# RWKV-7 chunk chain: the decayed old state added on VectorE in the state's update, in place of an identity product on TensorE

## Chip, cores, metric

One core of a Trainium2 chip. The metric is the device time of one execution in microseconds (us). The engines are called as in the profile: PE is TensorE (PEld its weight loads), DVE is VectorE, ACT is ScalarE, POOL is GpSimd, SP is SyncE, which here only issues DMAs.

## What is computed

One decoder layer on 512 tokens of 2048 channels, in fp32. Its sub-layer normalises and modulates x, projects it with a 2048 x 12416 matrix, mixes the time axis in two branches (RWKV-7 and a short convolution), gates both, projects them back and adds the result to x. What the change touches is the recurrence of RWKV-7, for 16 heads of 64 channels:

```python
def step(S, inp):
    r_t, w_t, k_t, v_t, kk_t, b_t = inp
    sa = jnp.einsum('bhvk,bhk->bhv', S, -kk_t)
    S = (S * w_t[:, :, None, :] + sa[..., None] * b_t[:, :, None, :]
         + v_t[..., None] * k_t[:, :, None, :])
    y_t = jnp.einsum('bhvk,bhk->bhv', S, r_t)
    return S, y_t
...
pa = pa + (shift_time(pa, 1) - pa) * mu_shift[l]     # pa: the projected columns of r, k, v
y_a = (rwkv7_mix(pa, ...) * jax.nn.silu(z_a)) @ p_a[l]
```

## The kernel before

The time axis is cut into NC = 8 chunks of 64 tokens, and the heads are taken in NP = 8 pairs; a pair fills the 128 partitions, one head on each half (the two slices in `halves`). Inside a chunk the recurrence is solved in closed form, and only the state goes from chunk to chunk. The generator `chunks(j, ...)` does this for pair j, and its loop over c (lines 870 to 901) is the serial chain that the change is about. `SB` holds two state buffers in SBUF, and each step reads S0 and writes S1. A step consists of these parts:

- `o1` (a 128 x 128 corner of PSUM bank tag "pc") is GK·VB (L877) plus AR·S0 (L879). AR·S0 is the first instruction that needs the new state.
- `o2` (PSUM bank tag "py") is Kt·VB (L883) plus ident·S0 (L885), the old state passed through an identity matrix so that it lands in the accumulator.
- ACT copies the two diagonal 64 x 64 blocks of o1 to `UB` (L888), and PE adds Z·UB to o2 (L890).
- ACT writes S1 as o2 times `end`, the decay over the chunk, in two 64 x 64 blocks (L895).

Each of these fp32 products stands in the trace as two rows of PE. The chain's steps 1 to 6 have the identity product (48 in all), steps 1 to 7 have AR·S0 (56 in all).

All of this runs inside a large dense projection: `dense()` (L1018 to L1044) multiplies h with the projection matrix, 128 x 512 columns at a time (L1036), from weights that ACT and POOL split into a high and a low part (`high`, `low`). A planner written in the kernel merges the streams: it steps a clock `now` by the books' cost of each PE instruction (`spend`), lets each side generator run when its time has come, and writes the instructions down in that order, one queue for each engine. `run(engine, cost, ...)` (L422) books an operation on ACT, DVE or POOL and writes it down at most SOON = 1.2 us ahead; its line L428 is therefore the line of nearly all work on these engines, and the text goes by the names of the tiles. After an operation that PE needs, a generator waits for its booked end plus HOP + SURE = 0.2 + 0.6 us before it writes the PE instruction down. Work of the next pair (`prepare`, `invert`) uses DVE at the same time as the chain of this pair: `invert` is a long row of small dependent DVE operations with names `invt`, `Xg`, `M`.

Of the kernel before, what the change touches and what calls it, by code (L numbers as in the profile page):

```python
# [11 lines left out]
AF = mybir.ActivationFunctionType  # L12
ALU = mybir.AluOpType
# [12 lines left out]
NC = T // C  # L26
# [50 lines left out]
def trunk(ctx: ExitStack, tc: tile.TileContext, xT_d, x_d, prm_d, crow_d, ada1_d, ada2_d, rows_d, w_d, lora_d, pa_d, pb_d,  # L77
          wo_d, out_d):
    nc = tc.nc
    V, A, G, TE, S = nc.vector, nc.scalar, nc.gpsimd, nc.tensor, nc.sync  # L80
# [26 lines left out]
    ident = cst.tile([P, P], F32, name="ident")  # L107
# [78 lines left out]
    with tc.tile_pool(name="ap", bufs=1) as ap, tc.tile_pool(name="psa", bufs=1, space=PSUM) as psa:  # L186
# [189 lines left out]
        while units or opened:  # L376
# [3 lines left out]
            if u is None and units and len(opened) < NOPEN:  # L380
                b, t, k0, n = units[0]
# [8 lines left out]
            b, t, ps, k0, n, i = u  # L390
# [20 lines left out]
    with tc.tile_pool(name="rp", bufs=1) as rp, tc.manual_schedule(engines=ALL):  # L411
# [6 lines left out]
        def spend(t):  # L418
            nonlocal now
            now += t  # L420

        def run(eng, cost, f, *args, **kw):  # L422

            two = eng in ("POOL", "DVE2")
            e = eng[:3] if eng == "DVE2" else eng
            while busy[e] > now + SOON:
                yield busy[e] - SOON
            f(*args, **kw)  # L428
            t = max(now, busy[e])
            if two:  # L430
                while port and port[0][1] <= now:
                    port.pop(0)
                for b, c in port:
                    if b < t + cost and t < c:
                        t = c
                port.append((t, t + cost))
                port.sort()
            busy[e] = t + cost
            return busy[e] + HOP
# [11 lines left out]
        def take(tag, name, n=T):  # L451
            while books[tag][0][0] is None or books[tag][0][0] > now:
                yield now + 0.25 if books[tag][0][0] is None else books[tag][0][0]
            books[tag].pop(0)
            book = [None]
            books[tag].append(book)
            return bank(tag, name, n), book

        def four(ps):
            return ps.rearrange("p (a b) -> p a b", a=4)  # L460
# [358 lines left out]
        def chunks(j, AR, GB, GK, bon, end, vpad, solved, **_):  # L819
# [24 lines left out]
            for c0, m in ((0, 4), (4, 4), (8, 1)):  # L844
# [6 lines left out]
                for h, b in enumerate(halves):  # L851

                    k0, k1 = max(c0 + h - 1, 0), min(c0 + m + h - 1, NC)
                    if k0 < k1:
                        w0 = k0 + 1 - h - c0
                        t = yield from run("ACT", 0.38, A.activation, VB[b, k0:k1, b], pv[b, w0:w0 + k1 - k0, b], AF.Copy)
# [13 lines left out]
            for c in range(NC):  # L870
                if c % 4 == 0:
                    p1, b1 = yield from take("pc", f"p1{n}_{c}")
                    p2, b2 = yield from take("py", f"p2{n}_{c}")
                    p1, p2 = four(p1), four(p2)
                o1, o2 = p1[:, c % 4, :], p2[:, c % 4, :]
                S0, S1 = SB[:, c % 2, :], SB[:, (c + 1) % 2, :]
                TE.matmul(o1, GK[:, c, :], VB[:, c, :], start=True, stop=(c == 0))  # L877
                if c:
                    TE.matmul(o1, AR[:, c, :], S0, start=False, stop=True)  # L879
                spend(0.44)  # L880

                if c < NC - 1:
                    TE.matmul(o2, Kt[:, c, :], VB[:, c, :], start=True, stop=False)  # L883
                    if c:
                        TE.matmul(o2, ident, S0, start=False, stop=False)  # L885
                    spend(0.44)
                for b in halves:
                    t = yield from run("ACT", 0.22, A.activation, UB[b, b], o1[b, b], AF.Copy)  # L888
                yield t + SURE
                TE.matmul(o2, Z[:, c, :], UB, start=(c == NC - 1), stop=True)  # L890
                spend(0.22)
                yield now + SUM
                if c < NC - 1:
                    for b in halves:
                        t = yield from run("ACT", 0.3, A.activation, S1[b, b], o2[b, b], AF.Copy, scale=end[b, c:c + 1])  # L895
                if c % 4 == 3:
                    for h in range(NH):
                        b, o = halves[h], halves[1 - h]
                        b1[0] = yield from run("ACT", 0.38, A.activation, yt[o, c - 3:c + 1, :], p1[o, :, b], AF.Copy)
                        b2[0] = yield from run("ACT", 0.38, A.activation, y2[o, c - 3:c + 1, :], p2[o, :, b], AF.Copy)  # L900
                yield t + SURE
# [166 lines left out]
        for i in range(NFULL):  # L1068
            for t, f in USES:
                due.append([0.0, f(i, first[t + i], [None])])  # L1070
        sides = [[g, 0.0] for g in (
            high(), low(), loader(), uses(soon), uses(due),
            side("chunks", lambda j: "solved" in ops[j] and "bon" in ops[j], lambda j: chunks(j, **ops[j])),
            side("ops", paced, lambda j: prepare(j, rkv[j], ops[j])),
            side("inv", lambda j: at["made"] > j, lambda j: invert(j, out=ops[j], **ops[j])),
# [270 lines left out]
```

## Time and profile before

| | |
|---|---|
| three runs | 1649.26, 1649.77, 1641.44 us (median 1649.26) |
| the profiled execution | 1647.3 us, of which the span of its instructions 1645.0 us |
| PE busy | 1610.1 us (98%) |
| DVE, ACT, POOL busy | 887.9 (54%), 654.5 (40%), 808.7 us (49%) |
| dense stage with the chains of the eight pairs | about 199 to 1257 us of the span |

The busy time of PE is the union of its rows, whose ends are modelled, so the pitch from the start of one row to the start of the next says more about cost than the length of a row. Times in a timeline count from the start of the span. The arrow in brackets names what ended the idle time of the engine.

### The profile page before, as it was taken

What the parts mean: (1) busy time and instruction counts of PE and PEld (TensorE: products, weight loads), DVE (VectorE), ACT (ScalarE), POOL (GpSimd) and SP (SyncE); (2) the same over time, 40 slices, a digit from 0 to 9 for tenths busy, and PEclk for the clock granted to TensorE, in tenths of its full rate; (3) what the DMA queues carried; (4) which work ended last, traced back from release to release, by engine and by line L of the source; (5) the groups of instructions that cost most, each with busy time, mean ns of one, the idle gap of its engine ahead of it and who ended that gap; (6) DMA issues with size and microseconds to landing.
All of it is one profiled execution on the core that took longest, in us unless ns stands there. A gap on an engine that the chain in (4) does not pass through costs nothing. (4 is left out here: it accounts for less than half of the span.)

```text
span 1645.0 us, 23157 instructions
## 1 busy us (share of the span) xinstructions
PE 1610.1 (98%) x8248; PEld 1325.5 (81%) x8248; DVE 887.9 (54%) x1548; ACT 654.5 (40%) x1363; POOL 808.7 (49%) x649
## 2 busy tenths in 40 slices
PE   6999999999999999999999999999999999999997
PEld 2778878888888888888888888888887887888885
DVE  3898287863868736826927687340201344544405
ACT  4555352424545235335345452344423223323411
POOL 1599565553434533544534445333444445775421
PEclk6999999999999999999999999999999999999998
DMA  7986334333322333343333234433443776665704
GB/s 259 396 324 256 91 106 124 103 103 100 95 87 82 102 110 87 102 116 97 115 102 101 77 98 120 113 108 97 136 152 109 233 239 191 204 208 171 239 26 154
DMA packets 138885, 235.72 MB, mean 143 GB/s; under 512 B 34833, under 2 KB 43665, under 8 KB 134673
## 3 DMA queue, kind: packets, MB, share of 16 engines
q1 hardware_dynamic: 138624, 234.15, 45.2%
q8 instruction: 65, 1.06, 0.3%
q14 instruction: 50, 0.41, 0.1%
q10 hardware_dynamic: 146, 0.09, 0.0%
HBM read 214.79 MB, written 19.14 MB: 142 GB/s over the span
## 5 line engine op out<-in xcount | busy, mean ns | idle before, releaser
L428 POOL TENSOR_TENSOR wL_c<-raw_c,wH_c 128x512 fp32r<-128x512 f32 x324 | 438.1, 1353 | 544.9 <-ACT wH_c L428 504.4
L1036 PE MATMUL ps_c<-hH,wL_c 128*128 128x512 f32 x1296 | 512.5, 395 | 0.6 <-POOL wL_c L428 0.6
L1036 PE MATMUL ps_c<-hH,wH_c 128*128 128x512 f32 x1296 | 512.8, 396 | 0.0
L1036 PE MATMUL ps_c<-hL,wH_c 128*128 128x512 f32 x1296 | 512.8, 396 | 0.0
L428 ACT ACTIVATE wH_c<-raw_c 128x512 fp32r<-128x512 f32 x324 | 204.3, 631 | 410.3 <-PE ps_c L1036 285.4
L1036 PEld LDWEIGHTS ps_c<-hH,wL_c 128*128 128x128 f32 x1296 | 243.8, 188 | 48.1 <-POOL wL_c L428 1.1
L1036 PEld LDWEIGHTS ps_c<-hH,wH_c 128*128 128x128 f32 x1296 | 243.7, 188 | 47.7
L1036 PEld LDWEIGHTS ps_c<-hL,wH_c 128*128 128x128 f32 x1296 | 243.7, 188 | 46.7
L149 POOL TENSOR_TENSOR fL<-fraw,fH 128x512 fp32r<-128x512 f32 x56 | 80.0, 1437 | 61.8 <-ACT fH L148 61.7
L428 DVE TENSOR_TENSOR invt<-M,Xg 128x60 f32<-128x60 f32 (+24 forms) x248 | 87.2, 351 | 42.3 <-DMA M<-s 34.6
L149 POOL TENSOR_TENSOR oL<-wo,oH 128x512 fp32r<-128x512 f32 x48 | 66.2, 1386 | 59.9 <-ACT oH L148 58.5
L160 PE MATMUL fps<-hH,fH 128*128 128x512 f32 x224 | 88.5, 395 | 4.1 <-ACT hH L259 4.1
L161 PE MATMUL fps<-hL,fH 128*128 128x512 f32 x224 | 88.5, 395 | 1.9 <-DVE hL L262 1.9
L162 PE MATMUL fps<-hH,fL 128*128 128x512 f32 x224 | 88.2, 394 | 1.7 <-POOL fL L149 1.7
L428 DVE TENSOR_TENSOR Xg<-Xg,invt 128x60 f32<-128x60 f32 (+24 forms) x248 | 83.9, 338 | 8.0
L428 DVE TENSOR_TENSOR GG<-pg,gmask 128x512 f32<-128x512 f32 x32 | 22.1, 692 | 109.5 <-PE pg L730 109.5
L245 DVE SCALAR_TENSOR_TENSOR ada<-ada,csr 128x2048 f32<-128x2048 f32 x32 | 72.6, 2276 | 13.9 <-PE csr L273 13.9
L160 PE MATMUL po<-oH,mH 128*128 128x512 f32 x192 | 74.7, 389 | 0.0
L161 PE MATMUL po<-oL,mH 128*128 128x512 f32 x192 | 74.7, 389 | 0.0
L162 PE MATMUL po<-oH,mL 128*128 128x512 f32 x192 | 74.7, 389 | 0.0
L148 ACT ACTIVATE oH<-wo 128x512 fp32r<-128x512 f32 x64 | 38.4, 627 | 74.1 <-PE po L162 46.7
L149 POOL TENSOR_TENSOR wL_pb<-raw_pb,wH_pb 128x512 fp32r<-128x512 f32 x32 | 41.3, 1292 | 49.4 <-ACT wH_pb L148 49.4
(268 smaller groups left out, 2599.5 us busy)
## 6 DMA issues: line engine op xcount, KB each, us to landing
raw_c<-in_w_dram SPq DMA_DIRECT2D x324, 256.0 KB, 2.7
ada<-in_ada_dram SPq DMA_DIRECT2D x32, 1024.0 KB, 8.8
gr<-in_ada_dram SPq DMA_DIRECT2D x64, 256.0 KB, 4.4
wo<-in_wo_dram SPq DMA_DIRECT2D x64, 256.0 KB, 3.7
fraw<-in_w_dram SPq DMA_DIRECT2D x56, 256.0 KB, 4.1
raw_pb<-in_pb_dram SPq DMA_DIRECT2D x32, 256.0 KB, 2.7
raw_pa<-in_pa_dram SPq DMA_DIRECT2D x32, 256.0 KB, 2.8
th_s<-th SPq DMA_DIRECT2D x30, 256.0 KB, 2.0
```

Of the source, the lines that this page charges most:

```text
L148: A.activation(H, src, AF.Copy)
L149: eng.tensor_tensor(L, src, H.bitcast(F32), ALU.subtract)
L160: TE.matmul(ps, wH, xH, start=start, stop=False)
L161: TE.matmul(ps, wH, xL, start=False, stop=False)
L162: TE.matmul(ps, wL, xH, start=False, stop=stop)
L245: V.scalar_tensor_tensor(ada[j, i], ada[j, i], 0.5, csr, ALU.mult, ALU.mult, accum_out=accs[j][:, i:i + 1])
L428: f(*args, **kw)
L1036: TE.matmul(ps, w[:, i, :], x[k], start=(k == k0 and x is hH and w is H), stop=(k == KT - 1 and w is L))
```

## The change

The identity product L885 goes. The old state is decayed on its own: ACT scales S0 by `end` into S1, the full 128 x 128 buffer in one instruction (steps 1 to 6, written down right behind the copies to UB), and DVE then adds the rest in place, S1 = o2 · end + S1, in two 64 x 64 blocks. In step 0, where there is no old state, DVE writes S1 = o2 · end. ACT's two blocks of L895 are thereby gone in all seven steps. The books change with it: 0.22 us for each product, and in step 0 the second product that was booked and did not exist is no longer booked.

```diff
-                spend(0.44)
+                spend(0.44 if c else 0.22)
 
                 if c < NC - 1:
                     TE.matmul(o2, Kt[:, c, :], VB[:, c, :], start=True, stop=False)
-                    if c:
-                        TE.matmul(o2, ident, S0, start=False, stop=False)
-                    spend(0.44)
+                    spend(0.22)
                 for b in halves:
                     t = yield from run("ACT", 0.22, A.activation, UB[b, b], o1[b, b], AF.Copy)
+                if 0 < c < NC - 1:
+                    yield from run("ACT", 0.4, A.activation, S1, S0, AF.Copy, scale=end[:, c:c + 1])
                 yield t + SURE
                 TE.matmul(o2, Z[:, c, :], UB, start=(c == NC - 1), stop=True)
                 spend(0.22)
                 yield now + SUM
                 if c < NC - 1:
                     for b in halves:
-                        t = yield from run("ACT", 0.3, A.activation, S1[b, b], o2[b, b], AF.Copy, scale=end[b, c:c + 1])
+                        e = end[b, c:c + 1]
+                        if c:
+                            t = yield from run("DVE", 0.28, V.scalar_tensor_tensor, S1[b, b], o2[b, b], e, S1[b, b], ALU.mult,
+                                               ALU.add)
+                        else:
+                            t = yield from run("DVE", 0.28, V.tensor_scalar, S1[b, b], o2[b, b], e, None, ALU.mult)
```

On PE, in pair 2 at step 5, the kernel before has this (p1 and p2 are the banks of o1 and o2, GG0 and ZK hold GK, Z and Kt, VY holds VB):

```order
L877 MATMUL p1_2_4_5960<-VY_3422,GG0_1766 128x128
L879 MATMUL p1_2_4_5960<-SB_1768,AR_2_4357 128x128
L883 MATMUL p2_2_4_5969<-VY_3422,ZK_3436 128x128
L885 MATMUL p2_2_4_5969<-SB_1768,ident_77 128x128
L1036 MATMUL ps_c12_5912<-hL6_760,wH_c12_1_5816 128x512
L1036 MATMUL ps_c12_5912<-hH6_759,wL_c12_1_5827 128x512
L1036 MATMUL ps_c12_5912<-hH7_869,wH_c12_1_5816 128x512
L1036 MATMUL ps_c12_5912<-hL7_870,wH_c12_1_5816 128x512
L1036 MATMUL ps_c12_5912<-hH7_869,wL_c12_1_5827 128x512
L1036 MATMUL ps_c12_5912<-hH8_977,wH_c12_2_5861 128x512
L1036 MATMUL ps_c12_5912<-hL8_978,wH_c12_2_5861 128x512
L890 MATMUL p2_2_4_5969<-UB_1769,ZK_3436 128x128
```

On PE at the same step the changed kernel has this:

```order
L877 MATMUL p1_2_4_5984<-VY_3422,GG0_1766 128x128
L879 MATMUL p1_2_4_5984<-SB_1768,AR_2_4354 128x128
L883 MATMUL p2_2_4_5985<-VY_3422,ZK_3436 128x128
L1041 MATMUL ps_c12_5907<-hL8_978,wH_c12_2_5866 128x512
L1041 MATMUL ps_c12_5907<-hH8_977,wL_c12_2_5878 128x512
L1041 MATMUL ps_c12_5907<-hH9_1069,wH_c12_2_5866 128x512
L1041 MATMUL ps_c12_5907<-hL9_1070,wH_c12_2_5866 128x512
L1041 MATMUL ps_c12_5907<-hH9_1069,wL_c12_2_5878 128x512
L1041 MATMUL ps_c12_5907<-hH10_1156,wH_c12_2_5866 128x512
L890 MATMUL p2_2_4_5985<-UB_1769,ZK_3436 128x128
```

The block is one product shorter, and six dense products stand between it and Z·UB where seven stood (L1036 has become L1041).

On DVE, in the inversion of pair 3, which runs beside the chain of pair 2, the kernel before has only the inversion's own pairs of operations:

```order
L428 TENSOR_TENSOR invt_3_14_6004<-M_3_5739,Xg_3_5740 128x68
L428 TENSOR_TENSOR Xg_3_5740<-Xg_3_5740,invt_3_14_6004 128x17x4
L428 TENSOR_TENSOR invt_3_15_6018<-M_3_5739,Xg_3_5740 128x64
L428 TENSOR_TENSOR Xg_3_5740<-Xg_3_5740,invt_3_15_6018 128x16x4
L428 TENSOR_TENSOR invt_3_16_6028<-M_3_5739,Xg_3_5740 128x75
L428 TENSOR_TENSOR Xg_3_5740<-Xg_3_5740,invt_3_16_6028 128x15x5
```

On DVE the changed kernel has this there:

```order
L428 TENSOR_TENSOR invt_3_14_5996<-M_3_5727,Xg_3_5728 128x68
L428 TENSOR_TENSOR Xg_3_5728<-Xg_3_5728,invt_3_14_5996 128x17x4
L428 TENSOR_TENSOR invt_3_15_6000<-M_3_5727,Xg_3_5728 128x64
L428 SCALAR_TENSOR_TENSOR SB_1768<-p2_2_4_5985,end_2_3870,SB_1768 64x64 x2
L428 TENSOR_SCALAR a_4_5974<-a_4_5974 128x512
L428 TENSOR_TENSOR Xg_3_5728<-Xg_3_5728,invt_3_15_6000 128x16x4
L428 TENSOR_TENSOR invt_3_16_6027<-M_3_5727,Xg_3_5728 128x75
L428 TENSOR_TENSOR Xg_3_5728<-Xg_3_5728,invt_3_16_6027 128x15x5
```

The two blocks of the state's update now stand in the middle of a dependent pair of the inversion. They wait for Z·UB on PE and for ACT's scaled copy, and the rest of the inversion waits behind them.

On ACT, in pair 2, the kernel before has a copy to UB and an update of SB in each step:

```order
L428 ACTIVATE wH_c20_1_5996<-raw_c20_1_5918 128x512
L428 ACTIVATE SB_1768<-p2_2_4_5969,end_2_3900 64x64 x2
L428 ACTIVATE UB_1769<-p1_2_4_5960 64x64 x2
L428 ACTIVATE wH_c20_2_6033<-raw_c20_2_5920 128x512
L428 ACTIVATE SB_1768<-p2_2_4_5969,end_2_3900 64x64 x2
```

On ACT the changed kernel has there:

```order
L428 ACTIVATE wH_c20_2_6021<-raw_c20_2_5928 128x512
L428 ACTIVATE UB_1769<-p1_2_4_5984 64x64 x2
L428 ACTIVATE SB_1768<-SB_1768,end_2_3870 128x128
L428 ACTIVATE wH_c20_3_6055<-raw_c20_3_5952 128x512
L428 ACTIVATE lm12_6070<-ps_c12_5907,prm_75 128x512
```

The scaled copy now directly follows UB and waits for nothing of PE beyond what UB waited for.

## Rows read from the trace of the kernel before

**Rows 1.** From the page: busy time, share and instructions of each engine, then the busy tenths of PE and the granted clock in 40 equal slices of the span.

```profile
PE 1610.1 (98%) x8248; PEld 1325.5 (81%) x8248; DVE 887.9 (54%) x1548; ACT 654.5 (40%) x1363; POOL 808.7 (49%) x649
...
PE   6999999999999999999999999999999999999997
...
PEclk6999999999999999999999999999999999999998
```

**Rows 2.** Busy time of each engine in four stretches: the start of the dense stage, the stretch with all eight chains, the rest of the dense stage, and what follows it. Columns: length, then busy us (and instructions) of PE, PEld, DVE, ACT, POOL, then granted clock, DMA share, GB/s.

```profile
190.00:398.00 208.00, 206.71 (x1018) 171.27 (x1017) 137.50 (x204) 78.96 (x145) 112.53 (x92) 1.00 0.35 105
398.00:1170.00 772.00, 771.91 (x4498) 648.65 (x4497) 447.31 (x921) 347.33 (x801) 341.82 (x282) 1.00 0.34 100
1170.00:1256.00 86.00, 86.00 (x407) 71.04 (x407) 9.56 (x21) 24.75 (x42) 41.38 (x32) 1.00 0.49 150
1256.00:1645.00 389.00, 374.27 (x1644) 307.56 (x1642) 159.44 (x244) 112.91 (x204) 187.42 (x137) 0.99 0.58 181
```

**Rows 3.** Timeline of PE through one step of the chain (pair 2) and to the first products of the next step: start, length, engine, line, what.

```profile
641.32 0.39 PE L1036 MATMUL ps_c<-hH,wH_c 128*128 128x512 f32 x1
641.55 0.38 PE L877 MATMUL p<-VY,GG 128*128 128x128 f32 x2
641.77 0.39 PE L879 MATMUL p<-SB,AR 128*128 128x128 f32 x2
641.99 0.39 PE L883 MATMUL p<-VY,ZK 128*128 128x128 f32 x2
642.22 0.39 PE L885 MATMUL p<-SB,ident 128*128 128x128 f32 x2
642.36 0.48 PE L1036 MATMUL ps_c<-hL,wH_c 128*128 128x512 f32 x1
642.67 0.40 PE L1036 MATMUL ps_c<-hH,wL_c 128*128 128x512 f32 x1
...
644.04 0.38 PE L890 MATMUL p<-UB,ZK 128*128 128x128 f32 x2
...
646.35 0.38 PE L877 MATMUL p<-VY,GG 128*128 128x128 f32 x2
646.57 0.39 PE L879 MATMUL p<-SB,AR 128*128 128x128 f32 x2
```

**Rows 4.** Groups of PE's instructions by line (rows, busy us, mean ns of a row, idle us before them): the product that goes.

```profile
L885 PE MATMUL p<-SB,ident 128*128 128x128 f32 x96 | 18.6, 275 | 0.0
```

**Rows 5.** Timeline of ACT in the same step: the copies to UB and the update of the state.

```profile
642.19 0.46 ACT L428 ACTIVATE UB<-p 64x64 f32<-64x64 f32 x2 [0.73 <-PE p L879]
...
644.46 0.63 ACT L428 ACTIVATE SB<-p,end 64x64 f32<-64x64 f32 x2 [0.22 <-PE p L890]
```

**Rows 6.** The step with the least time between the end of the state's update and the product that reads it (pair 7): timelines of ACT and of PE.

```profile
1155.16 0.62 ACT L428 ACTIVATE SB<-p,end 64x64 f32<-64x64 f32 x2
```
```profile
1156.97 0.39 PE L879 MATMUL p<-SB,AR 128*128 128x128 f32 x2
```

**Rows 7.** Timelines of DVE and of POOL in the step of rows 3, around the end of Z·UB.

```profile
644.28 0.23 DVE L428 TENSOR_TENSOR invt<-M,Xg 128x70 f32<-128x70 f32 x1
644.55 1.22 DVE L428 TENSOR_TENSOR Xg<-Xg,invt 128x70 f32<-128x70 f32 x1
645.80 0.23 DVE L428 TENSOR_TENSOR invt<-M,Xg 128x65 f32<-128x65 f32 x1
```
```profile
644.32 1.35 POOL L428 TENSOR_TENSOR wL_c<-raw_c,wH_c 128x512 fp32r<-128x512 f32 x1 [2.02 <-ACT wH_c L428]
```

**Rows 8.** Groups of DVE's instructions by shape, in the stretch with the eight chains (count, busy us, mean ns of one, idle us before and its releaser).

```profile
L428 DVE TENSOR_TENSOR GG<-pg,gmask 128x512 f32<-128x512 f32 x24 | 16.6, 692 | 84.3 <-PE pg L730 84.3
L428 DVE TENSOR_TENSOR BK<-rk,lw 64x512 f32<-64x512 f32 x12 | 12.6, 1048 | 0.0
...
L428 DVE SCALAR_TENSOR_TENSOR st<-st 128x8 f32<-128x8 f32 x42 | 11.4, 270 | 1.4
...
L428 DVE TENSOR_TENSOR invt<-M,Xg 128x28 f32<-128x28 f32 x14 | 2.6, 188 | 0.5
```

**Rows 9.** Groups of ACT's instructions by shape in the same stretch, and the one group with the decay's own tile, read by that tile (shortest, median and longest ns).

```profile
L428 ACT ACTIVATE wH_c<-raw_c 128x512 fp32r<-128x512 f32 x227 | 143.4, 632 | 251.8 <-PE ps_c L1036 166.1 <-POOL wL_c L428 40.5 <-issue 36.5
L428 ACT ACTIVATE SB<-p,end 64x64 f32<-64x64 f32 x112 | 34.6, 309 | 36.2 <-PE p L890 34.8
```
```profile
L428 ACT ACTIVATE end<-dec x8: 197/198/215, 225.7 to 975.1; 128x8 f32<-128x8 f32 x8
```

**Rows 10.** Busy time of the engines in the eight stretches in which a chain runs (columns as in rows 2): the first, the last, and the sum of all eight.

```profile
399.00:441.00 42.00, 42.00 (x221) 35.78 (x220) 32.33 (x84) 24.10 (x65) 18.05 (x16) 1.00 0.30 84
...
1132.00:1171.00 39.00, 39.00 (x208) 33.23 (x207) 0.53 (x1) 18.85 (x53) 14.15 (x11) 1.00 0.28 83
sum 334.00, PE 334.00 PEld 285.36 DVE 191.17 ACT 183.60 POOL 132.27; mean PE 41.75 PEld 35.67 DVE 23.90 ACT 22.95 POOL 16.53
```

## The prediction

> **What bounds the kernel now.** I read the engines' shares first, then the busy time by stretch, then PE's timeline through one step of the chain, and last what the other engines do in that step.
>
> PE is busy 98% of the span at the full granted clock [rows 1]. An average says little about one stage, so the stretch with the eight chains comes next: PE is busy 771.91 of 772.00 us there, and 86.00 of 86.00 in the dense work that follows [rows 2]. ACT (347 us) and POOL (342 us) are busy less than half of the 772 us, DVE 447. So nothing that the other engines do now reaches PE there.
>
> Modelled ends can make a row look busy that isn't, so the pitch decides. In the step of pair 2 the four small products start at 641.55, 641.77, 641.99 and 642.22, one each 0.22 us, and the dense rows around them go at 0.23 (641.32 to 641.55) [rows 3]. The whole block, from L877's start to the second dense product behind it, takes 642.67 − 641.55 = 1.12 us; less one dense pitch of 0.23 that is 0.89 for four products, 0.22 each. The first dense pitch behind the block is long (0.31), but the last small product's is short by the same amount, so the switch from one kind to the other costs nothing that the removal of one product would alter.
>
> The chain itself is not the bound. The new state is ready at 644.46 + 0.63 = 645.09, and AR·S0, which reads it, starts at 646.57 [rows 3, 5]: 1.48 us of cushion, filled with dense products. The least cushion of the 56 is 1156.97 − 1155.78 = 1.19 us [rows 6]. After the last chain the dense work goes on for 86 us more [rows 2], so a chain that takes some us longer doesn't end the kernel later either.
>
> **The change part by part.**
>
> *The identity product goes.* Its 96 rows are 48 products (two rows each), with no idle time before them [rows 4]. PE is the engine that sets the stage's length, and each product holds it for a pitch of 0.22 us (0.2225 from the block above): 48 × 0.2225 = **10.7 us** less, all of it on the path. The length of the row would give more, 48 × 0.39 = 18.7, but that length overlaps the next row's start and is only an upper end; zero is the lower end, if something else took PE's place as the bound. I take the pitch.
>
> *ACT loses the two blocks of the update and gains the scaled copy.* It loses 112 × 0.309 = 34.6 us [rows 9]. A copy of 128 x 128 is not in the trace; it lies between the 0.198 us of a 128 x 8 copy and the 0.632 of a 128 x 512 one, and I take 0.31, as for the 64 x 64 blocks that also read a scale from SBUF: 48 × 0.31 = 15 us (10 to 30). ACT gets 20 us freer (5 to 25), and it is off the path: worth nothing. The copy stands behind UB, which waits for PE's L879; what is queued behind it on ACT is the split of the next weights, at most 0.63 us later per step. PE's need of these is covered, since ACT is busy only 183.60 of the 334 us of the chains [rows 10]. The copy itself must be done before Z·UB ends: UB ended at 642.65, and Z·UB starts at 644.04 [rows 3, 5], which leaves room for the copy and one split of 0.63.
>
> *DVE gains 112 blocks of 64 x 64.* None of this kind is in the trace. The ends are 0.19 us (the smallest operation of the inversion) and 0.69 us (128 x 512 out of PSUM); nearest in shape is the 0.27 us of a scalar_tensor_tensor on 128 x 8 [rows 8]. With 0.27 the sum is 30 us (21 to 77), 3.8 us for each chain. DVE is busy 191.17 of the 334 us in which chains run and 32.33 of 42 in the fullest [rows 10]. It fits, so as throughput this costs nothing. The time from Z·UB to the finished state stays what it is: two blocks on ACT took 0.63 us, two on DVE take about 0.54.
>
> *The wait moves to another queue.* This is the part that can cost. DVE takes its work in order; the update now stands between operations of the next pair's inversion, and AR·S0 waits for it, and all dense work of PE behind AR·S0 with it. In the step of rows 3, DVE was in the inversion when Z·UB ended, and one operation that takes 0.23 us took 1.22, while POOL's subtraction ran from 644.32 to 645.67 [rows 7]: it was held for about 1.0 us. Had the update stood behind that one, it would have started at 645.80 and ended at about 646.35, still 0.2 us ahead of AR·S0. So one held operation is covered by the cushion, and two in a row are not; two would end the update at about 647.6 and hold PE for 1.0 us. The planner books POOL's holds as well, and in the trace no wait for DVE shows on PE in the stretch of the chains, though PE reads DVE's products there too. I put this at 0 to 1.5 us in all, 0.5 as the value. The other way round, what is queued behind the update on DVE (the inversion, products taken out of PSUM) waits for PE's Z·UB. The inversion has the rest of a chain's period to catch up, and a PSUM bank of the dense stream is needed only a tile later (48 products of 0.23, 11 us); I put this at nothing.
>
> The update itself has one input in PSUM and one in SBUF. Operations of that kind show no hold on average: 692 ns for GG from pg and gmask, against 1048 ns for BK, half as many partitions with both inputs in SBUF [rows 8]. By the Trainium skill, "SBUF — State Buffer", section "Who interferes with whom", a DVE instruction with at most one SBUF input, outside its two-port modes, does not contend with GpSimd, while one with two SBUF inputs does. The trace agrees; were the update held like the inversion's operations, each could cost 1.0 us more and the chance of the slower case below would have to be doubled.
>
> *The order.* Step by step PE does the same work less one product. The books are shorter by that product and by the one that step 0 booked without having it, so everything behind is written down somewhat earlier against the other engines; the planned distances behind DVE and ACT stay HOP + SURE. I cost it at nothing; a moved dense product that finds its weights late would show as a wait on POOL, and POOL is busy 341.82 of 772 us [rows 2].
>
> **The sum.** On the profiled execution: span 1645.0 − 10.7 + 0.5 = 1634.8, and with the 2.3 us around the span 1637.1 us. That execution (1647.3) lies 2 us under the median of the three runs (1649.26) and inside their spread (1641.44 to 1649.77); from the median the same sum would be 1639. I predict **1637**, a gain of 10.2 us or 0.6%.
>
> **The rivals.**
>
> *Late on DVE, in part.* In some steps the update stands behind two held operations. For it speaks that the inversion's operations are of the kind that is held [rows 7, 8] and that DVE's share is highest in the chains' stretches; against it the cushion of 1.19 us or more in all 56 steps. With 5 of 56 steps at 1.0 us the time is 1636.6 + 5 = 1642.
>
> *Slower: DVE becomes the chain's clock.* The same mechanism in many steps: PE stands at AR·S0, with the whole dense stream behind it. It decides from 11 steps on (11 × 1.0 = the 10.7 gained), and is slower by more than 0.5% from 19 on. With 24 of the 56 the time is 1636.6 + 24 = 1661. Against it: in the last pair DVE has nothing else to do (0.53 us busy in 39) [rows 10], no PE row in the stretch waits for DVE now, and two holds must follow each other within 2 us, while POOL is busy less than half the time.
>
> *Hidden.* The identity product filled time that PE would have spent anyway, and the change does not do what it says: 1647. The row that speaks for it is PEld, busy only 648.65 of the 772 us [rows 2]; against it stand the equal pitches of 0.22 us with no gap. The Trainium skill, "Perfetto Trace Analysis", section "Identifying the Most-Contended Engine", calls matmul busy time no good measure of the distance to the roofline and wants the share of weight loads looked at instead. By that rule PE had a reserve of 16% in this stretch, and taking work off it might give nothing; the trace's starts say otherwise.
>
> **How the numbers follow.** The bound at which a measurement of this kernel can tell a change is about 0.5%, 8.2 us; the forecast lies only 2 us beyond it. Chances: forecast 0.74 (of it 0.06 that reads as under 0.5%), late in part 0.13, hidden 0.06, slower 0.07 (of it 0.01 within 0.5%). So faster by over 0.5%: 0.74 − 0.06 = 0.68; within: 0.06 + 0.13 + 0.06 + 0.01 = 0.26; slower: 0.06. The range starts at the fastest run less the full gain, 1641.4 − 10.7, or 1630 with rounding down, and goes past the partial case with some of the runs' spread, to 1645. It leaves out the hidden and the slower case (0.13), and a little of the spread at each end.
>
> **What would show it.** Right: PE's stretch of dense stage ends 10 to 11 us earlier, the line of the identity product is gone, its neighbours keep a pitch of 0.22, and PE has no wait for DVE or ACT in the chains; SB's blocks stand on DVE with 0.2 to 0.3 us each and wait for PE's Z·UB. Wrong: PE idle before AR·S0, released by DVE's SB, with inversion operations of over 1.2 us ahead of it; or the same dense end as before with longer pitches. A cushion under 0.5 us in many steps would say that the forecast was near its edge.

## The result and the profile after

The changed kernel takes 1638.27 us (median of 20 runs, 1632.31 to 1644.00) against 1649.43 (20 runs, 1641.44 to 1652.45); the ratio is 0.9945, with a 95% interval of 0.993 to 0.996. The medians alone would give 0.993, the means (1638.1 against 1647.0) 0.995: single times of one kernel spread over 11 us and lie in groups, so a median can fall into either. The profiled execution took 1641.01 us, its span 1639.2. Some 6 us of such a spread can lie ahead of the changed stage (last section), so the kernels are compared below by the length of the dense stage: from the start of the first dense product to the start of the last. Each length comes from one profiled execution and from starts printed to 0.1 us, so a difference is good to 0.1 or 0.2 us; two runs below with the same code in this stage both had 1045.3 us. Three single executions of the experiments, two with the product put back and one with PE kept occupied, took 3.7 to 4.2 ms and are left out of all ratios and medians.

These are the first and the last group of dense products by line: shortest, median and longest ns, then the start of the group's first and last row. Before:

```profile
L1036 PE MATMUL ps_c<-hH,wH_c x1296: 387/389/501, 199.3 to 1255.9; 128*128 128x512 f32 x186
...
L1036 PE MATMUL ps_c<-hH,wL_c x1296: 387/389/501, 199.8 to 1256.4; 128*128 128x512 f32 x186
```

After:

```profile
L1041 PE MATMUL ps_c<-hH,wH_c x1296: 387/389/501, 201.2 to 1248.5; 128*128 128x512 f32 x186
...
L1041 PE MATMUL ps_c<-hH,wL_c x1296: 387/389/504, 201.6 to 1248.9; 128*128 128x512 f32 x186
```

The stage went from 1057.1 us (199.3 to 1256.4) to 1047.7 (201.2 to 1248.9), 9.3 us less. The other 3.5 us between that and the spans' 5.8 lie outside, in code that the change does not touch: the stage began 1.9 us later and the rest after it took 1.6 us longer. In both parts the granted clock fell to half for some 3.4 us in the changed kernel (around 49 and 1366 us) and not in the kernel before; such a stretch costs about 1.6 us (below). The second of them, columns as in rows 2:

```profile
1366.40:1370.00 3.60, 3.60 (x9) 2.71 (x10) 1.30 (x2) 1.49 (x3) 1.27 (x1) 0.53 0.28 80
```

Busy time of the engines over the span (beside [rows 1]), and in the stretch with the chains (beside [rows 2]; columns as there):

```profile
PE 1602.3 (98%) x8152; PEld 1317.0 (80%) x8152; DVE 929.5 (57%) x1660; ACT 638.8 (39%) x1299; POOL 812.0 (50%) x649
```
```profile
398.00:1170.00 772.00, 770.90 (x4436) 645.50 (x4435) 487.43 (x1029) 332.52 (x733) 349.27 (x286) 1.00 0.36 102
```

PE has 96 rows less, DVE 112 more, ACT 64 less. PE is now idle for 1.1 of the 772 us, where it had 0.09: small, but new. PE's timeline through a step of pair 2 (beside [rows 3]):

```profile
641.86 0.39 PE L1041 MATMUL ps_c<-hH,wH_c 128*128 128x512 f32 x1
642.09 0.38 PE L877 MATMUL p<-VY,GG 128*128 128x128 f32 x2
642.30 0.39 PE L879 MATMUL p<-SB,AR 128*128 128x128 f32 x2
642.53 0.39 PE L883 MATMUL p<-VY,ZK 128*128 128x128 f32 x2
642.67 0.48 PE L1041 MATMUL ps_c<-hL,wH_c 128*128 128x512 f32 x1
642.99 0.40 PE L1041 MATMUL ps_c<-hH,wL_c 128*128 128x512 f32 x1
```

The block, up to the second dense product behind it, now takes 642.99 − 642.09 = 0.90 us where it took 1.12, and the neighbours keep their pitch of 0.21 to 0.23. The new work, read by its tile (shortest, median, longest):

```profile
L428 DVE SCALAR_TENSOR_TENSOR SB<-p,end,SB x96: 265/284/293, 407.6 to 1177.6; 64x64 f32<-64x64 f32 x96
L428 ACT ACTIVATE SB<-SB,end x48: 401/403/406, 406.0 to 1175.9; 128x128 f32<-128x128 f32 x48
L428 DVE TENSOR_SCALAR SB<-p,end x16: 266/284/294, 403.1 to 1152.2; 64x64 f32<-64x64 f32 x16
```

No update took longer than 0.294 us, though 61 of the 112 ran while POOL was at work: none was held. These are the waits of PE that have DVE as their releaser and that are new in the stage (total us, times, longest):

```profile
PE y L926 <- DVE VY L428: 0.7, 1, 0.7
...
PE p L879 <- DVE SB L428: 0.3, 1, 0.3
```

The second is in pair 0. Timelines of DVE and of PE there:

```profile
434.56 1.16 DVE L428 TENSOR_TENSOR invt<-M,Xg 128x28 f32<-128x28 f32 x1
...
437.24 0.39 DVE L428 COPY M<-Xg 32x256 f32<-32x256 f32 x1
...
438.55 1.03 DVE L428 COPY M<-Xg 32x256 f32<-32x256 f32 x1
439.59 0.58 DVE L428 SCALAR_TENSOR_TENSOR SB<-p,end,SB 64x64 f32<-64x64 f32 x2
```
```profile
439.60 0.38 PE L877 MATMUL p<-VY,GG 128*128 128x128 f32 x2
440.32 0.46 PE L879 MATMUL p<-SB,AR 128*128 128x128 f32 x2 [0.34 <-DVE SB L428]
```

The update ended at 440.17, behind a copy of the inversion that took 1.03 us; AR·S0 would have started at 439.82 and started at 440.32, 0.5 us late. (The view counts a wait from the modelled end of the row before, so it shows 0.34.) Two operations were held in this step, the copy (1.03 us, 0.39 for its like) and one of the inversion (1.16 us, 0.19 on average for its shape before [rows 8]), each beside a subtraction of POOL (from 438.03 and from 434.37 us), and DVE had no idle time between them and the update.

The products that turn y at the end of a pair's chain waited too, in pair 5: they started 1.08 us behind the dense product before them, where 0.32 is usual, so 0.76 us were lost. Here no update of SB was near, since the chain had ended. Ahead of y on DVE, two small operations took 1.42 us beside a subtraction of POOL (such a pair took 0.37 us a little later). DVE, then POOL:

```profile
1006.97 1.42 DVE L428 SCALAR_TENSOR_TENSOR st<-st 128x8 f32<-128x8 f32 x2
```
```profile
1007.08 1.29 POOL L428 TENSOR_TENSOR wL_c<-raw_c,wH_c 128x512 fp32r<-128x512 f32 x1 [0.78 <-ACT wH_c L428]
```

### The profile page after: what moved, and what is told of

It is laid out like the page before. It is cut to its first block, busy times and chain, and to the rows that moved or that the text cites. A ratio compares the mean times of both kernels' runs of the same rounds, so it can differ in the third digit from the quotient of the medians.

```text
span 1639.2 us, 23135 instructions
## 1 busy us (share of the span) xinstructions
PE 1602.3 (98%) x8152; PEld 1317.0 (80%) x8152; DVE 929.5 (57%) x1660; ACT 638.8 (39%) x1299; POOL 812.0 (50%) x649
## 5 line engine op out<-in xcount | busy, mean ns | idle before, releaser
L1041 PE MATMUL ps_c<-hH,wL_c 128*128 128x512 f32 x1296 | 513.3, 396 | 0.7 <-POOL wL_c L428 0.7
L1041 PE MATMUL ps_c<-hH,wH_c 128*128 128x512 f32 x1296 | 513.6, 396 | 0.0
L1041 PE MATMUL ps_c<-hL,wH_c 128*128 128x512 f32 x1296 | 512.0, 395 | 0.0
L1041 PEld LDWEIGHTS ps_c<-hH,wL_c 128*128 128x128 f32 x1296 | 243.8, 188 | 48.4 <-POOL wL_c L428 1.1
L1041 PEld LDWEIGHTS ps_c<-hL,wH_c 128*128 128x128 f32 x1296 | 243.8, 188 | 47.2
L1041 PEld LDWEIGHTS ps_c<-hH,wH_c 128*128 128x128 f32 x1296 | 243.8, 188 | 46.8
L428 DVE TENSOR_TENSOR invt<-M,Xg 128x60 f32<-128x60 f32 (+24 forms) x248 | 91.9, 370 | 7.9
L428 DVE TENSOR_TENSOR Xg<-Xg,invt 128x60 f32<-128x60 f32 (+24 forms) x248 | 89.0, 359 | 7.9
```

Source lines behind the costliest of these rows:

```text
L1041: TE.matmul(ps, w[:, i, :], x[k], start=(k == k0 and x is hH and w is H), stop=(k == KT - 1 and w is L))
```

## The experiments

My theory: PE is the bound of the stage, the 48 products are worth their pitch there, and the move to DVE costs only the odd wait. Rivals: the move itself gains or costs (ACT freer, DVE later), the planner's shorter books did it, or DVE sets the chain's pace.

**The product put back, without its effect** (a product on a tile of zeros; the edit also makes and clears that tile and moves a small tile of the last stage, `ssq`, to another pool, which is not shown):

```diff
                     TE.matmul(o2, Kt[:, c, :], VB[:, c, :], start=True, stop=False)
-                    spend(0.22)
+                    if c:
+                        TE.matmul(o2, ident, ZT, start=False, stop=False)
+                    spend(0.44 if c else 0.22)
```

> The changed kernel with an identity product put back in steps 1 to 6 of each chain, on a tile of zeros, so that it adds nothing; ACT's scaled copy and DVE's update stay. If the whole gain is PE's pitch, 48 x 0.22 us, the dense stage (first to last dense product) grows by 10.7 us against the changed kernel, from 1047.7 to 1058 (+-1), and the time is that of the kernel before within 0.3% (about 1648). If the move from ACT to DVE brought or cost something of its own, the stage differs from the 1057.1 of before by that: under 1055 for a gain of the move, over 1060 for a cost.

The stage took 1061.1 us (194.4 to 1255.5), the time was 1.0039 of before (1.0014 to 1.0064). That is over the 1060 that I had written down for a cost of the move. The excess has its place:

```profile
PE y L929 <- DVE VY L428: 2.5, 1, 2.5
```

One wait for y in pair 5, and behind it PE runs at half clock for 3.4 us (below). Together they are worth about 4 us (2.5 and 1.6); without them, by this estimate, the stage would be 1057, that of before. No update of SB was near here either. Three small operations on y's sums took this long beside three of POOL without a gap between them:

```profile
978.39 3.55 DVE L428 TENSOR_SCALAR st<-st 128x8 f32<-128x8 f32 x3
```

So putting the 48 products back takes the gain away, and what the order adds can be as large as 4 us.

**DVE's update alone, with the identity product kept** (kernel before):

```diff
-t = yield from run("ACT", 0.3, A.activation, S1[b, b], o2[b, b], AF.Copy, scale=end[b, c:c + 1])
+t = yield from run("DVE", 0.28, V.tensor_scalar, S1[b, b], o2[b, b], end[b, c:c + 1], None, ALU.mult)
```

> The kernel before with one edit: the two blocks of the state's update run on DVE, as o2 times end, in place of ACT; the identity product stays and there is no scaled copy. If DVE's place in the chain costs only the odd wait, the stage is 1057.1 + 0 to 1.5 us and the time within 0.3% of before. If the rival of DVE as the chain's clock held, PE would wait for SB in tens of steps and the stage grow by 5 us or more.

The stage took 1057.9 us (194.5 to 1252.4), 0.8 more than before; the ratio is 1.0019 (1.0000 to 1.0038). PE waited once for SB:

```profile
PE p L879 <- DVE SB L428: 0.8, 1, 0.8
```

PE also waited 0.3 us at a turn of y. The move from ACT to DVE gains nothing, although ACT is freed of its blocks of the update, and costs one wait in 56 steps. The rival of DVE as the chain's clock falls for this load.

**The old books:**

```diff
-                spend(0.44 if c else 0.22)
+                spend(0.44)
...
-                    spend(0.22)
+                    spend(0.44)
```

> The changed kernel with the planner's books as before (0.44 us for each block, though PE has one product less): the planner then believes PE to be later than it is by 0.22 us in each step. If the gain is PE's work and not the order, the stage is 1047.7 +-1.0 and the time within 0.3% of the changed kernel. If the tighter books brought part of it, the stage is 1050 or more; if they caused the two waits that came new (0.3 us at AR.S0, 0.7 at y), these go and the stage is 1046.5 to 1047.

The stage took 1052.5 us (193.1 to 1245.6), 4.8 more than the changed kernel, with the same instructions; ratio 0.9983 (0.9959 to 1.0007). That is what I had written down for "the tighter books brought part of it", but the next run shows otherwise. (In step 0 of each chain the old books count two products that are not there, one in each block.) PE lost 2.5 us at the turn of y in pair 5. Timelines of DVE, POOL and PE ahead of it:

```profile
980.79 3.56 DVE L428 TENSOR_SCALAR st<-st 128x8 f32<-128x8 f32 x3
```
```profile
980.50 1.30 POOL L428 TENSOR_TENSOR wL_c<-raw_c,wH_c 128x512 fp32r<-128x512 f32 x1 [2.08 <-ACT wH_c L428]
981.77 1.30 POOL L428 TENSOR_TENSOR sL<-sq,sH 128x512 fp32r<-128x512 f32 x1
983.03 1.30 POOL L428 TENSOR_TENSOR wL_c<-raw_c,wH_c 128x512 fp32r<-128x512 f32 x1
```
```profile
985.46 0.39 PE L1041 MATMUL ps_c<-hL,wH_c 128*128 128x512 f32 x1
988.30 1.15 PE L926 MATMUL y<-ident,VY 64*64 64x64 f32 x32 [2.46 <-DVE VY L428]
...
991.39 0.63 PE L1041 MATMUL ps_c<-hH,wL_c 128*128 128x512 f32 x1
991.82 0.63 PE L1041 MATMUL ps_c<-hH,wH_c 128*128 128x512 f32 x1
```

Three operations on 128 x 8, booked at 0.17 each, took 3.56 us while three subtractions of POOL followed each other without a gap; they end at 984.35 and 984.33. No update of SB was near: this chain had ended. The Trainium skill, "SBUF — State Buffer", section "Who interferes with whom", lists tensor_scalar among the operations that can contend with GpSimd for the port pair that the two share, when their operands meet the conditions of a two-port mode. The trace fits that: in this kernel every such operation on `st` that met no operation of POOL took 0.17 us, and of those that met one the longest took 1.25. The planner books them without POOL in mind. After the wait, dense products went at a pitch of 0.43 for a while; the windows (columns as in rows 2) give the clock:

```profile
980.00:985.00 5.00, 5.00 (x23) 4.13 (x22) 4.76 (x10) 2.72 (x5) 3.83 (x3) 1.00 0.27 83
985.00:989.80 4.80, 2.34 (x38) 1.76 (x37) 3.87 (x12) 0.51 (x2) 2.20 (x4) 0.99 0.39 109
989.80:993.20 3.40, 3.40 (x10) 2.62 (x9) 1.55 (x3) 0.72 (x2) 1.28 (x1) 0.51 0.02 5
```

Having stood for some 2.5 us, PE got half the clock (1.2 GHz) for 3.4 us, which cost another 1.6 us: eight products at 0.43 in place of 0.23. Whether a wait has this sequel is taken up in the last section.

**The old books, y later** (no instruction changed, the turn of y is written down 2.4 us later):

```diff
-            yield SURE + (yield from run("DVE2", 0.7, V.tensor_tensor, yt, yt, rs.unsqueeze(2).to_broadcast([P, NC, C]),
+            yield 3.0 + (yield from run("DVE2", 0.7, V.tensor_tensor, yt, yt, rs.unsqueeze(2).to_broadcast([P, NC, C]),
```

> The run with the old books, with the products that turn y written down 2.4 us later behind DVE. If the wait of 2.5 us for VY and the half clock behind it made that run's stage 1052.5, it falls by 3.5 to 4 us to 1048.5 (+-0.7). If the old books themselves cost it, it stays at 1051 to 1053.

```profile
L1041 PE MATMUL ps_c<-hH,wH_c x1296: 387/389/502, 201.2 to 1247.2; 128*128 128x512 f32 x186
...
L1041 PE MATMUL ps_c<-hH,wL_c x1296: 387/389/502, 201.7 to 1247.6; 128*128 128x512 f32 x186
```

1046.4 us (201.2 to 1247.6): 6.1 less, more than the 3.5 to 4 expected, and a stage below the 1048.5 (+-0.7). Two waits of 0.5 us at AR·S0 and at Kt·VB went with the moved order as well, which accounts for part of the difference. So the old books cost nothing; the waits did. No wait for SB or VY is left on PE, and the stage is 10.7 us under that of before. The ratio is 0.995 (0.9929 to 0.9971).

**The changed kernel with both distances** (y as above, and AR·S0 later, at the end of a step):

```diff
-                yield t + SURE
+                yield t + 2 * SURE
             at["chain"] = j + 1
```

> The changed kernel with the planner's distances grown at the two places where PE waited for DVE in it: AR.S0 is written down 0.6 us later behind the booked end of the update, and the products that turn y 2.4 us later behind the last DVE operation on y. No instruction is added. If these waits are what the removal's 10.7 us lost, the stage falls from 1047.7 to 1046.4 (+-0.5) and no row of PE waits for SB or VY. If the order alone moves the stage by us, it lands elsewhere, 1045 to 1052.

The stage is 1045.3 (195.6 to 1240.9), and with the turn of y of the last pair, which here comes right behind the last dense product (1.1 us), 1046.4. PE waits for neither SB nor VY. The time is 1633.61 us (6 runs, 1631.27 to 1638.42), ratio 0.9924 (0.9901 to 0.9948): the best of the runs, 1.3 us shorter in the stage than the changed kernel, with the intervals of the two overlapping.

**The same two distances in the kernel before:**

> The kernel before, with the identity product and the update on ACT, and with the same two distances as in the run with the grown distances (0.6 us more behind the update, 2.4 us more ahead of the products that turn y). It shows what the distances bring without the change. If they only take away waits for DVE, of which the kernel before has a few tenths of a us, the stage is 1056.5 to 1057.5, so that 10.3 to 11 us remain between it and 1046.4. If the distances themselves bring us, the stage is 1055 or less.

The stage is 1056.8 us (199.3 to 1256.1), 0.3 less than before, the ratio 1.0007 (0.9985 to 1.0028). The distances bring nothing of their own. Between the two kernels without waits for SB or VY lie 1056.8 − 1046.4 = 10.4 us: that is the worth of the 48 products, 0.217 us each.

**The update twice as long on DVE:**

```diff
-                if 0 < c < NC - 1:
-                    yield from run("ACT", 0.4, A.activation, S1, S0, AF.Copy, scale=end[:, c:c + 1])
...
-    t = yield from run("DVE", 0.28, V.scalar_tensor_tensor, S1[b, b], o2[b, b], e, S1[b, b], ALU.mult, ALU.add)
+    yield from run("DVE", 0.28, V.tensor_tensor, S1[b, b], o2[b, b], S0[b, b], ALU.add)
+    t = yield from run("DVE", 0.28, V.tensor_scalar, S1[b, b], S1[b, b], e, None, ALU.mult)
```

> The changed kernel with the whole update on DVE: o2 plus S0, then that times end, two blocks each, so four operations of DVE a step (booked at 0.28 each) in place of two, and no scaled copy on ACT. If the cushion ahead of AR.S0 hides the update, the stage is 1047.7 + 0 to 2 us. If each step's update bounds the chain's readers on PE, 0.5 us more in each of 48 steps shows as up to 24 us.

```profile
PE p L879 <- DVE SB L428: 2.4, 4, 1.0
```

The stage took 1050.8 us (193.2 to 1244.0), 3.1 more: a little over the 0 to 2 expected, and far from 24. In four steps of 56 PE waited for the update; ratio 0.9956 (0.9935 to 0.9976). This form needs nothing of ACT in the update and no scaled copy, and still keeps most of the gain.

**The update delayed, in two doses** (an operation that waits for Z·UB, unbooked, once or three times ahead of each update):

```diff
                 if c < NC - 1:
+                    for _ in range(3):
+                        V.tensor_reduce(scr, o2.unsqueeze(1).to_broadcast([P, 4, P]), mybir.AxisListType.X, ALU.add)
                     for b in halves:
```

> The changed kernel with one extra DVE operation that nothing uses ahead of each of the 56 updates: a row sum over o2 read four times (128 x 512 out of PSUM, about 0.69 us), which waits for Z.UB as the update does and is not in the planner's books. If the cushion ahead of AR.S0 hides a late update, only the few steps with less than 0.7 us of cushion stall: the stage grows from 1047.7 to 1049 (+-1.5). If each late update reaches PE, 56 x 0.7 = 39 us.

> The same with three such operations (about 2.1 us) ahead of each update. In the changed kernel's trace the cushions of the 56 steps lie between 0.15 and 3.95 us; what 2.1 us would overshoot sums to about 20 us, so the stage grows to 1068 (1063 to 1075) with PE waiting for SB in some 30 steps: the rival of DVE as the chain's clock, forced. If the cushion did not matter, 56 x 2.1 = 118 us.

Waits of PE with one operation, then with three:

```profile
PE y L929 <- DVE VY L428: 4.1, 3, 3.1
...
PE p L880 <- DVE SB L428: 1.2, 2, 0.8
```
```profile
PE p L880 <- DVE SB L428: 32.4, 33, 2.7
PE p L884 <- ACT VY L428: 5.2, 8, 1.0
PE y L929 <- DVE VY L428: 3.7, 3, 2.6
```

With one, the stage is 1055.6 us (194.4 to 1250.0), where I expected 1049: the cushion ahead of AR·S0 did hold (1.2 us in two steps, not 39), but the turn of y, which stands behind the same queue, lost 4.1 us and a stretch of half clock. With three it is 1105.5 (193.1 to 1298.6), where I expected 1063 to 1075. The number of steps that wait, 33, is as expected; the size is not, since I took the cushions of the changed kernel as fixed. DVE with 116 us more work hands each delay on to the next step and to y, and the granted clock fell to half three times in the stage. How much each of these adds was not taken apart. The form of the rival is right: with 2.1 us per step DVE becomes the chain's clock, and the kernel is slower than before (one run, 1689.98 us).

**POOL's hold in the books** (old books, with the four small tensor_scalar operations of y booked as `DVE2`, which the planner keeps clear of POOL; one of them. Two of the four stand in a helper that the normalisation of kk uses as well, so two longer operations of each pair are booked otherwise too):

```diff
-            yield from run("DVE", 0.17, V.tensor_scalar, m, m, 1.0 / HS, None, ALU.mult)
+            yield from run("DVE2", 0.17, V.tensor_scalar, m, m, 1.0 / HS, None, ALU.mult)
```

> The run with the old books, in which the products that turn y waited 2.5 us for DVE, with one edit to the books: the four small tensor_scalar operations of y's normalisation are booked like DVE's two-input operations, which the planner keeps clear of POOL's. No distance and no instruction changes. If POOL's hold on these operations made the wait (three of them took 3.56 us while POOL worked without a break), PE waits under 0.5 us for VY in every pair and the stage is 1046.5 to 1048.5. If the wait came from the amount of DVE's work, it stays and the stage is 1050 or more.

```profile
PE ps_c L1041 <- DVE v L428: 2.1, 1, 2.1
...
PE p L879 <- DVE SB L428: 1.7, 3, 1.2
...
PE y L926 <- DVE VY L428: 0.3, 1, 0.3
```

The wait for VY fell from 2.5 to 0.3 us, as it should if POOL's hold made it. But the stage is 1053.2 us (193.3 to 1246.5), outside the 1046.5 to 1048.5: the moved order made a new wait of 2.1 us for v elsewhere, with half clock behind it, and 1.7 us at AR·S0. DVE sat idle ahead of v for 5.6 us, waiting for ACT's lm; why ACT came late with it I did not trace. Nor did the books keep POOL away: 13 of the 32 small operations still met one of POOL's, and the longest took 1.23 us. So this run does not settle what the hold cost. That the hold exists, the traces show: over all thirteen runs none of these operations that met nothing of POOL took more than 0.18 us, and in each run the longest that did took 1.2 to 1.5.

**PE kept occupied at the start** (112 small products that nothing reads, in four places, on top of the grown distances):

```diff
+        for _ in range(40):
+            TE.matmul(warm, hsumr, hsumr, start=True, stop=True)
         columns(0, 0)
```

> The run with the grown distances, with 112 small products that nothing reads (128 x 128, fp32r) in PE's queue before and between the first products, where PE waits for the norm of x in the first 37 us. The dense stage is as in that run, 1046 with the last turn of y counted in. In the profiles so far the granted clock was at half for 27 us or for 10 to 14 us of the first 55, and the dense stage began 5 to 6 us later in the first case; single times of one kernel lie in two groups some 8 us apart. If the clock at the start makes these groups, PE's fuller start takes the longer fall away: the runs lie within 5 us and their median is 1627 to 1632. If not, median (1633.6) and spread stay, or the extra products delay the start by up to 5 us.

A miss: 1654.76 us, ratio 1.0054 (1.0035 to 1.0072), and the runs spread over 10 us as before. The stage is unchanged (1045.3 us, 219.5 to 1264.8), but it begins 24 us later than in the run without these products. PE's timeline:

```profile
40.79 8.77 PE L270 MATMUL warm<-hsumr 128*128 128x128 f32 x40
...
57.15 0.63 PE L162 MATMUL fps<-hH,fL 128*128 128x512 f32 x1
57.58 0.63 PE L160 MATMUL fps<-hH,fH 128*128 128x512 f32 x1
```

Each took 0.22 us, some 25 us in all, and held up the products that matter, and at 57 us the dense products behind them still went at a pitch of 0.43, that of half the clock (the record of the clock in this trace begins at 60.55 us; ahead of it the view prints 1.00).

## Why the prediction was right

- **PE bounds the stage, by its pitch.** Right. The stage fell by 9.3 us; between the kernels without waits for SB or VY it is 10.4 (1056.8 against 1046.4), for 10.7 predicted. The pitch read from one block, 0.2225 us, was 2 to 3% too long: 0.217 measured.
- **The range and the chance.** 1638.27 lies by the forecast of 1637. That it lies so near is in part luck: ten of the 20 times are 1632 to 1637, ten 1640 to 1644, and the median falls in the gap. The ratio of 0.9945 is just beyond the 0.5% at which I set the border, as the forecast said it would be. By the interval (0.993 to 0.996), faster by over 0.5% is likelier than not but not certain.
- **ACT's part is worth nothing.** Right in effect: with DVE's update alone, without the scaled copy, the stage is as before. The copy was mis-sized, 0.40 us against 0.31, and no wait for it shows on PE.
- **DVE's part fits.** Right: 0.284 us an update against 0.27 (31.7 us in all against 30), none held. DVE's busy time rose by 41.6 us, though: the inversion's pairs of operations (`invt`, `Xg`) took 9.8 us more over the span, and others moved both ways. One row was misread: DVE's share is not highest where chains run (191 of 334 us, 57%), but at the start of the dense stage (137.50 of 208 us, 66%) [rows 2, 10].
- **The wait moves to DVE.** Right: 0.5 us predicted, 0.5 measured at AR·S0 in one step of 56, with two held operations in that step, as the prediction asked (not one behind the other, but with no idle time between). Of the other 55 cushions one is 0.24 us and the rest are 1.20 or more. So the sign "no wait for DVE in the chains" failed by one step, within the term's 0 to 1.5 us.
- **The order costs nothing.** This step failed, though not by enough to show in the changed kernel's sum. Kernels with the same instructions had stages of 1046.4, 1047.7, 1052.5 and 1053.2 us: the planner's order decides what DVE is late with. In the two runs that lost 2.5 us at y, three of POOL's operations fell on DVE's small ones ahead of something PE needs. The place that I did not name is y: the products that turn it wait for DVE too, and lost 0.76 us in the changed kernel and 2.5 in those two, with no update of SB near. I had costed the order at nothing, with weights from POOL as the only thing that could come late; the price in these runs is 0 to 7 us and its place is DVE.
- **The slower rival** came true with 2.1 us of delay a step and not with 0.69; nothing between them was tried, and the delays were also work on DVE (116 and 39 us).
- **Hidden** falls: with the products put back the gain is gone, and between kernels without waits for SB or VY the products are worth 10.4 us.

## What to carry to other kernels

Where PE issues without a gap, a product is worth its pitch, and it can be had by giving its work to an engine that is idle half the time; read the pitch from starts, since rows overlap. Then look at what PE will wait for on the engine that takes the work, all of it and not only the moved operation: a queue in order makes everything behind it later. Where an order is planned from booked costs, measure a change by the stage's length and by its waits, since the same work in a slightly other order can differ by more than a small gain; a longer planned distance ahead of a consumer that nobody is in a hurry for is a cheap remedy, as 0.6 and 2.4 us were here.

## What the runs showed of the hardware

Two things were not expected. A wait of PE can cost more than itself: behind the 2.46 us at y, in the runs with the old books and with the product put back, the granted clock was half for 3.4 us, 1.6 us more. The length of the wait alone does not decide it. Behind the 2.12 us for v the clock fell too, and outside the dense stage behind 1.80 us in the changed kernel (at 1366 us); but with three operations of delay it stayed full behind a wait of 2.71 us that ended at 676.40 us:

```profile
676.40:680.00 3.60, 3.60 (x18) 3.03 (x19) 3.40 (x7) 2.97 (x8) 1.58 (x1) 1.00 0.00 0
```

In the dense stage, waits of 0.8 us and less had no such sequel. What else decides it stays open.

And the same program starts in more than one way. Busy time and clock (columns as in rows 2) in the kernel before, then in the run with the update twice as long on DVE, whose instructions in this part are the same:

```profile
10.00:23.00 13.00, 13.00 (x28) 2.31 (x26) 0.75 (x1) 4.88 (x9) 0.00 (x0) 0.70 1.05 393
...
35.00:54.00 19.00, 14.56 (x50) 10.95 (x51) 15.56 (x14) 10.97 (x23) 6.90 (x6) 0.80 0.80 301
```
```profile
10.00:23.00 13.00, 11.85 (x42) 3.15 (x40) 2.29 (x2) 7.21 (x13) 0.34 (x1) 1.00 1.04 388
...
35.00:54.00 19.00, 17.14 (x70) 13.53 (x69) 15.99 (x15) 12.44 (x26) 7.99 (x6) 0.94 0.98 391
```

With PE at half clock (1.2 GHz) in part of the first stretch, granted 0.70 on average, it does 28 rows there against 42, and the dense stage begins at 199.3 us against 193.2. The profiles show both kinds of start for different kernels, one execution each, so some 6 us of the spread between single times of one kernel can lie here, ahead of the changed code. The granted clock of single runs fits that: over the whole span the changed kernel's ten shorter times have 0.991 to 0.994, its ten longer ones 0.986 to 0.989. A few of the longest times of the kernel before have 0.997 or 0.998, which this does not explain. The attempt to fill PE's queue at the start did not bring the better one; what decides it stays open.
